# A hybrid mixer's values and keys turned to token order by VectorE's block transposes and transfers between partitions, in place of TensorE's transposes

## The chip, the core and the metric

The kernel runs on one core of one Trainium2 chip. The metric is the device time of one execution in microseconds (us). Three executions of the kernel before took 2284.95, 2286.54 and 2284.74 us; the median is 2284.95 us. The engines are called as in the profile: PE (TensorE, matmuls), PEld (its weight loads), DVE (VectorE), ACT (ScalarE), POOL (GpSimd) and SP (SyncE, which here only issues transfers).

## The reference

One step of a hybrid decoder layer for 256 new prompt tokens and 8 sample sequences of 4 tokens each, so 288 token columns. The model width is 2048. Every sub-layer is added to x:

```
x = x + 1/2 * post1(SwiGLU_1(pre1(x)))
x = x + post2(HybridMixer(pre2(x)))
x = x + 1/2 * post3(SwiGLU_2(pre3(x)))
```

The mixer multiplies its input by one large weight matrix, whose columns are split into queries, keys, values, decays and gates of two groups of heads: GLA (4 heads, 128 key and 256 value dimensions) and HGRN (8 heads, 128 and 128). Each head runs a linear recurrence:

```
S_t = diag(a_t) S_{t-1} + k_t^T v_t ;  o_t = q_t S_t
...
s_new = (jnp.exp(last[:, :, 0, :])[..., None] * s
         + jnp.einsum('bhsd,bhsv->bhdv', ki * jnp.exp(last - cum), vi))
```

The prompt begins from a zero state and each sample from a state that is given. The outputs are the new x for all tokens, and the final states of the prompt and of every sample. What matters for this change: the products need values `v` and keys `k` with the *token* on the partitions (the sum over tokens is the matmul's contraction), while the projection leaves them with the *feature* on the partitions. So values and keys have to be turned.

## The kernel before, in words

Activations lie transposed: a tile has 128 features on its partitions and 288 token columns (columns 0 to 255 are the prompt, 256 to 287 the samples). Weights stream from HBM as fp32 in units of 128 x 1024 elements (512 KB) through the class `Weights`: SP issues the load into one of three raw buffers (`RAW_BUFS`), ACT copies the unit to a rounded high part `wh` (line 95), DVE subtracts for the low part `wl` (line 96), and four such pairs are kept (`HL_BUFS`). A weight block of 128 x 128 takes three matmuls (lines 520, 521 and 522). The function `block` computes 512 output features from 16 contraction steps; one step is 4 x 3 = 12 matmuls, a block 192. After each step it calls `tick`, which may put other work into PE's stream; when a block ends, its four results are evacuated by the function `evac`.

There are three phases: the first SwiGLU (0 to 853 us of the profiled span), the mixer (854 to 1421) and the second SwiGLU (to the end). In the mixer the blocks come in this order: `qk0`, `v0`, `qk1`, `v1` (GLA's two pairs of heads), `hfq0`, `hi0`, `hfq1`, `hi1`, `hfq2`, `hfq3` (HGRN: decays and queries, and values), the gates, and the output projection `mo`. While they run, six scans (g0 and g1 of GLA, h0 to h3 of HGRN, each for two heads) go along as Python generators: `tick` steps the generator at the head of the list `gens` once per contraction step, and scans come one after another. A scan first works out decayed scores level by level, then turns keys (`key_t`, `key_e`), makes the prompt's output (`out`), the prompt's final state (`final`: matmuls on line 1108, a copy on ACT, line 1110, and a POOL transfer, line 1111), and goes through the samples (`halve`, `apart`, `sample`; the sample states leave by POOL, line 1147), then adds the parts up (`inter_a`, `inter_b`) and normalises (`norm_a` to `norm_c`).

The values' evacuation `ev_v` before: for each of the four results f, two DVE operations (lines 831 and 832) scale the prompt's columns into a tile y and the samples' columns, three times over, into a tile v3. A function `turn` is put on the list `turns`, which `tick` empties one at a time: it does three PE transposes by `by_token` (lines 810 and 811) into a PSUM tile `tp_v`, an ACT copy into `Vt` (line 839: prompt values by token, 128 tokens x 2), one into `V32` (line 840: the 32 sample tokens), and `stack` (an ACT copy, line 815, and a DVE subtraction, line 817) into `Vs`, which holds the sample values as high, low and high parts in its 96 partitions. Keys go the same way in `key_t` (three transposes into `tp_k`) and `key_e` (an ACT copy into `kd`, line 1076, and `stack` into `ks`).

The order of instructions on each engine is set when the program is built: a scheduler places them by priority and by a planner's costs, and `issue_after` pins some behind others. Transfers issued by SP and POOL each go round eight semaphores: a transfer waits until the one issued eight before it on the same queue has landed. Auxiliary PSUM tiles (`tp_v`, `tp_k`, `st` and the scores) share three buffers.

## Time and profile before

| | before |
|---|---|
| median of three executions | 2284.95 us |
| profiled execution, its own time | 2287.87 us |
| span of the profiled execution | 2286.1 us |
| granted TensorE clock (1 is full speed) | 0.998 |
| PE busy over the span | 2270.9 us (99%) |
| DVE / ACT / POOL busy | 1409.7 / 1045.5 / 57.5 us |
| mixer window, 854 to 1421: PE, DVE, ACT, POOL busy | 564.3, 450.0, 334.9, 44.9 us |

The profile is one execution. Its page gives the busy time of each engine, the busy share in 40 slices, the chain of work that ended last (followed back from the last instruction, by share of engine), and groups of instructions by line. A row of a group reads: line, engine, operation, output<-input by the program's names, shapes and count | busy us, mean ns of one | idle time of the engine just before them and what ended it. A row of a timeline reads: start in us, duration in us, engine, line, operation, names, shapes, count; where PE's matmuls overlap, their starts tell the pace. A row of the waits reads: engine, the waiting tile and line, what it waited for, us in total, times, longest.

### The profile page before, as it was taken

The page shows a single profiled execution, that of the slowest core. Times are in us where ns is not written, and L with a number is a line of the kernel's source. Part 1 is how long each engine was busy: PE and PEld are TensorE (multiplying, and loading weights), DVE is VectorE, ACT ScalarE, POOL GpSimd, SP SyncE. Part 2 cuts the span into 40 slices and gives each one's busy share as a digit, 9 for nine tenths or more (in the row PEclk, how much of TensorE's full clock was granted, in tenths as well). Part 3 has the DMA queues.
Part 4 walks back from the last instruction along what each step waited for, and adds up shares of the span by engine and source line. Part 5 has one row for each costly group of instructions (what it writes and reads, how often), then busy time and mean ns, then how long its engine had stood idle before and what let it go on. Part 6 is the DMA issues. An engine that isn't in the chain of part 4 may idle for free.

```text
span 2286.1 us, 42014 instructions
## 1 busy us (share of the span) xinstructions
PE 2270.9 (99%) x17224; PEld 2257.6 (99%) x17224; DVE 1409.7 (62%) x2319; ACT 1045.5 (46%) x1654; POOL 57.5 (3%) x104
## 2 busy tenths in 40 slices
PE   9999999999999999999999999999999999999998
PEld 9999999999999999999999999999999999999998
DVE  6545545554555468889889754844555455545545
ACT  6443333333334346555666654644333333333345
POOL 0000000000000002001000000100000000000000
PEclk9999999999999999999999999999999999999999
DMA  7555555555556545456565554455555555555553
GB/s 213 171 165 166 165 167 164 167 166 167 165 166 185 166 157 169 138 171 191 151 177 164 162 184 155 141 171 166 164 167 164 169 161 166 166 163 163 165 165 115
DMA packets 218560, 378.28 MB, mean 165 GB/s; under 512 B 15634, under 2 KB 55104, under 8 KB 218368
## 3 DMA queue, kind: packets, MB, share of 16 engines
q1 hardware_dynamic: 212560, 365.48, 53.4%
q0 software_dynamic: 3632, 9.94, 1.3%
q8 instruction: 135, 2.21, 0.4%
q10 hardware_dynamic: 2176, 0.18, 0.1%
q14 instruction: 57, 0.47, 0.1%
HBM read 363.75 MB, written 11.80 MB: 164 GB/s over the span
## 4 chain that ended last, share of the span: by engine, by line
PE 94%; DVE 3%; ACT 1%; DMA 1%; issue 0%; DVEq 0%; ACTq 0%; SPq 0%
PE gate L522 9%; PE gate L520 9%; PE gate L521 9%; PE up L522 8%; PE up L520 8%; PE up L521 8%; PE out L521 8%; PE out L522 8%; PE out L520 8%; PE hfq L520 2%; PE hfq L522 2%; PE mo L522 1%; PE mo L520 1%; PE mo L521 1%; PE hfq L521 1%; PE v L520 1%
## 5 line engine op out<-in xcount | busy, mean ns | idle before, releaser
L96 DVE TENSOR_TENSOR wl<-raw,wh 128x1024 fp32r<-128x1024 f32 (+1 forms) x674 | 821.9, 1220 | 631.8 <-ACT wh L95 629.7
L95 ACT ACTIVATE wh<-raw 128x1024 fp32r<-128x1024 f32 (+1 forms) x674 | 711.3, 1056 | 1018.4 <-PE gate L521 312.4
L520 PE MATMUL gate<-xh,wh 128*128 128x288 f32 x1660 | 489.2, 296 | 0.9 <-ACT wh L95 0.9
L522 PE MATMUL gate<-xh,wl 128*128 128x288 f32 x1660 | 489.0, 295 | 0.2 <-DVE wl L96 0.2
L521 PE MATMUL gate<-xl,wh 128*128 128x288 f32 x1660 | 485.6, 295 | 0.6 <-DVE xl L253 0.6
L521 PE MATMUL out<-hl,wh 128*128 128x288 f32 x1408 | 415.8, 295 | 0.0
L520 PE MATMUL out<-hh,wh 128*128 128x288 f32 x1408 | 415.6, 295 | 0.0
L522 PE MATMUL up<-xh,wl 128*128 128x288 f32 x1408 | 415.1, 295 | 0.0
L522 PE MATMUL out<-hh,wl 128*128 128x288 f32 x1408 | 414.9, 295 | 0.0
L520 PE MATMUL up<-xh,wh 128*128 128x288 f32 x1408 | 414.8, 295 | 0.1
L521 PE MATMUL up<-xl,wh 128*128 128x288 f32 x1408 | 414.6, 294 | 0.0
L520 PEld LDWEIGHTS gate<-xh,wh 128*128 128x128 f32 x1660 | 310.9, 188 | 1.8 <-ACT wh L95 1.1
L522 PEld LDWEIGHTS gate<-xh,wl 128*128 128x128 f32 x1660 | 311.5, 188 | 0.6 <-DVE wl L96 0.6
L521 PEld LDWEIGHTS gate<-xl,wh 128*128 128x128 f32 x1660 | 310.4, 188 | 1.0 <-DVE xl L253 0.8
L522 PEld LDWEIGHTS out<-hh,wl 128*128 128x128 f32 x1408 | 264.7, 188 | 0.0
L520 PEld LDWEIGHTS out<-hh,wh 128*128 128x128 f32 x1408 | 264.6, 188 | 0.0
L520 PEld LDWEIGHTS up<-xh,wh 128*128 128x128 f32 x1408 | 264.1, 188 | 0.5 <-ACT g L590 0.3
L521 PEld LDWEIGHTS out<-hl,wh 128*128 128x128 f32 x1408 | 264.5, 188 | 0.0
L521 PEld LDWEIGHTS up<-xl,wh 128*128 128x128 f32 x1408 | 264.2, 188 | 0.1
L522 PEld LDWEIGHTS up<-xh,wl 128*128 128x128 f32 x1408 | 264.2, 188 | 0.0
L650 DVE TENSOR_TENSOR y<-out,y 128x288 f32<-128x288 f32 x288 | 121.6, 453 | 104.2 <-PE out L522 101.4
L520 PE MATMUL hfq<-xh,wh 128*128 128x288 f32 x256 | 77.5, 303 | 0.0
(381 smaller groups left out, 2558.6 us busy)
## 6 DMA issues: line engine op xcount, KB each, us to landing
raw<-in_ffn_w_in_dram SPq DMA_DIRECT2D x351, 512.0 KB, 3.6
raw<-in_ffn_w_out_dram SPq DMA_DIRECT2D x176, 512.0 KB, 3.8
raw<-in_mix_w_in_dram SPq DMA_DIRECT2D x64, 512.0 KB, 3.7
raw<-in_mix_w_in_dram SPq DMA_DIRECT2D x96, 256.0 KB, 3.3
raw<-in_mix_w_out_dram SPq DMA_DIRECT2D x32, 512.0 KB, 3.8
out_dram<-s POOLq DMA_DIRECT2D x32, 256.0 KB, 3.4
s<-in_state_gla_dram SPq DMA_DIRECT2D x16, 256.0 KB, 4.4
s<-in_state_hgrn_dram SPq DMA_DIRECT2D x16, 256.0 KB, 3.4
```

Of the source, the lines that this page charges most:

```text
L95: i1 = self.nc.scalar.activation(h[:, c], raw[:, c], AF.Copy).ins
L96: i2 = self.nc.vector.tensor_tensor(l[:, c], raw[:, c], h[:, c].bitcast(F32), op=ALU.subtract).ins
L520: yield lambda: PE.matmul(dst, w[0][:, c:c + P], parts[0], start=start, stop=False)
L521: yield lambda: PE.matmul(dst, w[0][:, c:c + P], parts[1], start=False, stop=False)
L522: yield lambda: PE.matmul(dst, w[1][:, c:c + P], parts[0], start=False, stop=stop)
L650: V.tensor_tensor(y[k], ps, y[k], op=ALU.add)
```

## The change

Three things change.

1. Values. The sixteen y tiles become four groups of four (`yg`), so that the four results of a value block lie in one tile of 128 x 4 x 288. `ev_v` scales each result with one DVE operation. At the fourth it transposes the whole group in place in 32 x 32 blocks on DVE, and issues 36 transfers within the chip's own memory (18 on SP's queue, 18 on POOL's): for each of four blocks of partitions one into `V32` and eight into `Vt`, each moving 32 partitions x 4 x 32 elements in pieces of 128 bytes. The three PE transposes and the copies from PSUM go. The list `turns` gets two empty entries and one `turn` for the block, which makes `Vs` from `V32` with two ACT copies and a DVE subtraction of 32 x 512.
2. The prompt's keys. `keys_by_token`, called once in a scan behind `key_t(0)`, transposes both heads' keys in place on DVE (2 x 256 columns) and issues 32 POOL transfers into one `kd` tile. `key_t` keeps only the transpose for the samples' keys, and the ACT copy into `kd` goes.
3. The final states. `final(0)` and `final(1)` move from the first sample step of each head to the scan's end, behind `inter_a(1)` and `norm_a(1)`.

Over the whole program PE loses 72 transposes of 128 x 128 or 128 x 96 (48 `tp_v`, 24 `tp_k`); SP issues 72 more transfers and POOL 264 more.

```
-    y = [xpool.tile([P, T], F32, name=f"y{k}") for k in range(KT)]
+    yg = [xpool.tile([P, 4, T], F32, name=f"y{k}") for k in range(4)]
+    y = [yg[k // 4][:, k % 4, :] for k in range(KT)]
...
-            def ev_v(Vt, V32, Vs, y0=8):
+            def ev_v(Vt, V32, Vs, g=2):
+                vg = yg[g]
                 def ev(f, ps):
-                    vt = y[y0 + f]
-                    v3 = tmp.tile([P, 3, TS], F32, name="v3", tag="v3", bufs=4)
-                    V.tensor_tensor(vt[:, 0:TP], ps[:, 0:TP], rt[:, 0:TP], op=ALU.mult)
-                    V.tensor_tensor(v3, ps[:, TP:T].unsqueeze(1).broadcast_to([P, 3, TS]),
-                                    rt[:, TP:T].unsqueeze(1).broadcast_to([P, 3, TS]), op=ALU.mult)
-                    def turn():
-                        tp = auxtile("tp_v")
-                        by_token(tp, vt, v3.rearrange("p n t -> p (n t)"))
-                        c = slice(f * P, (f + 1) * P)
-                        S.activation(Vt[:, 0:2, c], tp[:, 0:TP].rearrange("p (t c) -> p t c", c=P), AF.Copy)
-                        S.activation(V32[0:TS, c], tp[0:TS, TP:TP + P], AF.Copy)
-                        stack(Vs[:, c], tp, TS)
-                    turns.append(turn)
+                    V.tensor_tensor(vg[:, f, :], ps, rt, op=ALU.mult)
+                    if f == 3:
+                        V.transpose(vg, vg)
+                        for b in range(4):
+                            rows, cols = slice(b * TS, (b + 1) * TS), slice(b * TS, (b + 1) * TS)
+                            queue = nc.sync if b % 2 else G
+                            queue.dma_start(V32[0:TS].rearrange("p (f c) -> p f c", c=P)[:, :, cols], vg[rows, :, TP:T])
+                            for t in range(2):
+                                for c in range(4):
+                                    c0 = t * P + c * TS
+                                    queue.dma_start(Vt[c * TS:(c + 1) * TS, t].rearrange("p (f c) -> p f c", c=P)[:, :, cols],
+                                                    vg[rows, :, c0:c0 + TS])
+                        turns.append(lambda: None)
+                        turns.append(lambda: None)
+                        turns.append(turn)
+                def turn():
+                    v = V32[0:TS, :]
+                    S.activation(Vs[0:TS, :], v, AF.Copy)
+                    V.tensor_tensor(Vs[TS:2 * TS, :], v, Vs[0:TS, :].bitcast(F32), op=ALU.subtract)
+                    S.activation(Vs[2 * TS:96, :], v, AF.Copy)
                 return ev
...
+                def keys_by_token():
+                    V.transpose(k[:, :, 0:TP], k[:, :, 0:TP])
+                    kd = sp[0].tile([P, 2, 2, P], F32, name="kd", tag="kd", bufs=1)
+                    for a in range(2):
+                        for b in range(4):
+                            src = k[b * TS:(b + 1) * TS, a, 0:TP].rearrange("p (t q c) -> p t q c", t=2, q=4)
+                            for c in range(4):
+                                G.dma_start(kd[c * TS:(c + 1) * TS, a, :, b * TS:(b + 1) * TS], src[:, :, c, :])
+                    return kd
                 def key_t(a):
                     tp = auxtile("tp_k")
-                    by_token(tp, k[:, a, :], K3[:, a].rearrange("p n t -> p (n t)"))
+                    PE.transpose(tp[0:96, TP:TP + P], K3[:, a].rearrange("p n t -> p (n t)"), ident)
                     return tp
                 def key_e(a, tp):
-                    kd = sp[0].tile([P, 2, P], F32, name="kd", tag="kd")
                     ks = sp[0].tile([96, P], F32R, name="ks", tag="ks")
-                    S.activation(kd, tp[:, 0:TP].rearrange("p (t c) -> p t c", c=P), AF.Copy)
                     stack(ks, tp, 2 * TS)
-                    kds[a] = kd, ks
+                    kds[a] = None, ks
...
                 tp = key_t(0)
+                kd = keys_by_token()
                 halve(0, 0)
...
-                        if b0 == 0:
-                            final(a)
                         sample(a, b0)
...
                     inter_a(a)
+                    if a == 1:
+                        final(0)
                     yield
                     inter_b(a)
                     norm_a(a)
+                    if a == 1:
+                        final(1)
```

More of the change, by code (lines that the diff above doesn't have):

```diff
@@ L1103, in final @@
                 def final(a):
-                    kd, vc = kds[a][0], Vt[:, :, a * dv:(a + 1) * dv]
+                    vc = Vt[:, :, a * dv:(a + 1) * dv]
                     ps = auxtile("st")
                     for t in range(2):
-                        PE.matmul(ps[:, 0:dv], kd[:, t, :], vc[:, t, :], start=t == 0, stop=t == 1)
+                        PE.matmul(ps[:, 0:dv], kd[:, a, t, :], vc[:, t, :], start=t == 0, stop=t == 1)
                     st = tmp.tile([P, dv], F32, name="st", tag="st", bufs=1)
@@ L1334, in mixer @@
                     vts[g] = vtiles(f"h{g}")
-                    block(f"hi{g}", KT, xrhs, ev_v(*vts[g], 8 + 4 * g), tick=tick)
+                    block(f"hi{g}", KT, xrhs, ev_v(*vts[g], 2 + g), tick=tick)
                 else:
```

## The prediction

> **What bounds the kernel now.** I read the page's busy totals first, then its chain, then the windows of the three phases, and last PE's own timeline around the steps that the change touches.

> ```profile
> span 2286.1 us, 42014 instructions
> PE 2270.9 (99%) x17224; PEld 2257.6 (99%) x17224; DVE 1409.7 (62%) x2319; ACT 1045.5 (46%) x1654; POOL 57.5 (3%) x104
> PE 94%; DVE 3%; ACT 1%; DMA 1%; issue 0%; DVEq 0%; ACTq 0%; SPq 0%
> ```

> PE is busy all through, and 94% of the chain that ended last is PE: the kernel is the sum of its matmuls. The next view gives each phase (first SwiGLU, mixer, second SwiGLU) by engine: PE, PE's weight loads, DVE, ACT, POOL.

> ```profile
> 0.00:853.00 853.00, 850.20 (x6403) 848.90 (x6404) 478.07 (x667) 351.60 (x446) 3.40 (x14) 1.00 0.57 171
> 854.00:1421.00 567.00, 564.31 (x4361) 554.69 (x4362) 449.99 (x975) 334.86 (x714) 44.86 (x71) 1.00 0.56 167
> ```

> VectorE is 79% busy in the mixer against 56% in the phase before. In the mixer PE idles under 3 us of 567, DVE has 117 us idle, ACT 232, POOL nearly everything. A change there can win only PE time that it removes, and lose whatever it makes PE wait for. PE's timeline (start, duration) shows what a turn of values costs:

> ```profile
> 918.68 0.29 PE L520 MATMUL qk<-xh,wh 128*128 128x288 f32 x1
> ...
> 919.47 0.38 PE L810 MATMUL tp_v<-ident,y 128*128 128x128 f32 x2
> 919.69 0.27 PE L811 MATMUL tp_v<-ident,v 128*96 128x128 f32 x1
> 919.72 0.38 PE L520 MATMUL qk<-xh,wh 128*128 128x288 f32 x1
> 919.93 0.30 PE L521 MATMUL qk<-xl,wh 128*128 128x288 f32 x1
> ```

> Starts count, since matmuls overlap. Six ordinary matmuls take 919.47 − 918.68 = 0.79 us, 0.132 each. The three transposes hold PE for 0.25 us (919.47 to 919.72), and the ordinary matmul behind them takes 0.21 to its successor, 0.08 too long: 0.33 us for a turn.

> ```profile
> 1085.94 0.38 PE L810 MATMUL tp_k<-ident,k_h 128*128 128x128 f32 x2
> 1086.15 0.27 PE L811 MATMUL tp_k<-ident,acc 128*96 128x128 f32 x1
> 1086.26 0.39 PE L1095 MATMUL o<-Dg,Vh 128*128 128x128 f32 x2
> ```

> A turn of keys: 0.32 us for three, of which the L810 pair (1085.94 to 1086.15) is 0.21 and the third, which stays, 0.11.

> **The change, part by part.**

> *PE.* 16 value turns (4 blocks by 4) go: 16 × 0.33 = 5.3 us. 12 key turns lose two of three: 12 × 0.21 = 2.5 us. Together 7.8 us, all on the bound. Bounds: from the durations, 48 tp_v records are 7.92 us busy and 36 tp_k 5.91 us (two thirds 3.9), which overlap each other; so above 11.8 us nothing, and by starts alone without the slow follower 4.0 + 2.5 = 6.5. I take 7.8. The `st` matmuls only move.

> *DVE and ACT.* These groups (count | busy, mean ns) carry the removed and the nearest added work:

> ```profile
> L831 DVE TENSOR_TENSOR y<-hi,rt 128x256 f32<-128x256 f32 x8 | 3.3, 418 | 0.0
> L832 DVE TENSOR_TENSOR v<-hi,rt 128x96 f32<-128x96 f32 x8 | 2.0, 251 | 0.0
> L817 DVE TENSOR_TENSOR Vsh<-tp_v,Vsh 32x128 fp32r<-32x128 f32 x8 | 2.3, 284 | 1.2 <-ACT Vsh L815 1.0
> L1297 DVE TENSOR_TENSOR z<-hfq,rt 128x288 f32<-128x288 f32 x16 | 7.1, 451 | 2.4 <-PE hfq L522 2.3
> L96 DVE TENSOR_TENSOR wl<-raw,wh 128x1024 fp32r<-128x1024 f32 (+1 forms) x674 | 821.9, 1220 | 631.8 <-ACT wh L95 629.7
> L839 ACT ACTIVATE Vh<-tp_v 128x256 f32<-128x256 f32 x8 | 3.0, 371 | 0.4 <-PE tp_v L811 0.3
> L840 ACT ACTIVATE vs<-tp_v 32x128 f32<-32x128 f32 x16 | 4.0, 251 | 0.0
> L815 ACT ACTIVATE Vsh<-tp_v 96x128 fp32r<-96x128 f32 x8 | 2.0, 252 | 0.0
> L1076 ACT ACTIVATE kd<-tp_k 128x256 f32<-128x256 f32 x12 | 4.5, 373 | 3.4 <-PE tp_k L811 3.4
> ```

> DVE loses 16 × (0.418 + 0.251 + 0.284) = 15.2 us and gains 16 evacuations of 128x288 at 0.451 = 7.2. No row shows a 32x32 block transpose. Its lower bound is L1297's slope: 32 columns more than L831 cost 33 ns, so 1152 columns 1.3 us and 512 columns 0.65; L96 gives 1.2 us per 1024 likewise. The upper bound is the small-operand price: 36 blocks and 16 blocks at L832's 251 ns each, 9 and 4 us. Being one instruction over a whole row of columns it is nearest to L96, so I take 1.4 us (four) and 0.65 (six), 9.5 us together, and four subtractions of 32x512 at about 0.65, 2.6. DVE: −15.2 + 7.2 + 9.5 + 2.6 = +4.1 us of 117 idle; at the upper bound +55. [...] ACT loses 16 × 0.874 + 12 × 0.373 = 18.5 and gains eight copies of 32x512 at some 0.6: −13.7. Neither is on PE's path.

> *DMAs.* Each of four value blocks sends 18 on SP's queue and 18 on POOL's; each of six scans sends 32 on POOL's. Rows for the issue cost, and for landing (KB each, us):

> ```profile
> 0.74 0.43 SPq L276 DMA_DIRECT2D xin<-in_x_prompt_dram  x1
> L1147 POOL DMA_DIRECT2D out_dram<-s x32 | 23.5, 733 | 62.6 <-DVE s L1145 52.8 <-DMA raw<-in_mix_w_in_dram 7.3 <-DVE k_h L1308 1.9
> L1111 POOL DMA_DIRECT2D out_dram<-st x12 | 6.6, 553 | 272.3 <-ACT st L1110 183.6 <-ACT hl L1122 71.8 <-DMA raw<-in_mix_w_in_dram 8.7
> 880.13 3.83 POOL L776 DMA_DIRECT2D y<-in_gla_w_gate_up_dram  x8 [21.16 <-DVE x L492]
> 884.53 2.02 POOL L776 DMA_DIRECT2D y<-in_gla_w_gate_up_dram  x4 [0.56 <-DMA y<-in_gla_w_gate_up_dram]
> out_dram<-st POOLq DMA_DIRECT2D x8, 64.0 KB, 2.0
> araw<-in_mix_w_in_dram ACTq DMA_DIRECT2D x1, 128.0 KB, 7.3
> ```

> POOL: 0.48 each in a burst (3.83 / 8), 0.55 once the ninth waits for the first to land (884.53 − 880.13 over 8). I take 0.55, the bounds being 0.48 and L1147's 0.733. So 18 take 9.9 us and 32 take 17.6. Landing: 2.0 (st) to 7.3 (the 128 KB load in small pieces); I take 2.5, nearest to the 16 KB pieces of `st`'s kind. SP: 18 × 0.43 = 7.7 us per block, ahead of the next weight load. What covers it: a split unit of 1024 columns feeds 24 matmuls, 24 × 0.132 = 3.2 us, and four split buffers (HL_BUFS) hold 12.7 us, three raw ones another 9.5. So 0 here, and 7.7 per block if those buffers happened to be empty.

> *The new waits.* (a) Values. In before the last evacuation of v0 is at 916.80 (L832), so the transpose is done near 918.5, and the tenth POOL DMA, the last that V32 needs, is issued by 924.0 and lands at 926.5. The third turn asks for it on ACT near 924.4. Behind it on ACT is the scan's R (L893), and behind that PE's first scores:

> ```profile
> 916.80 0.25 DVE L832 TENSOR_TENSOR v<-v,rt 128x96 f32<-128x96 f32 x1
> 924.37 0.36 ACT L839 ACTIVATE Vg<-tp_v 128x256 f32<-128x256 f32 x1
> 925.06 0.47 ACT L893 ACTIVATE R<-Q 128x288 f32<-128x288 f32 x1
> 928.75 0.94 PE L901 MATMUL sc<-R,k_g 128*128 128x128 f32 x7
> ```

> ACT stalls 2 us, makes two copies (1.2) and R (0.5): ready at 928.2, while PE, without four turns, asks at 928.75 less four turns of 0.33, 927.4. Stall 0.8; bounds 0 (landing 1.7 sooner) and 6 (landing 7.3). The other three blocks ask later after their evacuation; 0.2 together. (b) Keys. `final` moves to the scan's end, where kd is now asked. In the built order 122, 140, 149 and 168 ordinary matmuls lie between tp_k and the second `st` of h0 to h3, with some 5 us of scan matmuls among them: 21.0, 23.4, 24.6 and 27.1 us; for g0 and g1 far more. kd is there after 1.5 (DVE) + 32 × 0.55 + 2.5 = 21.6. Stall 0.6 at h0, none elsewhere. At 0.48 none at all; at 0.733 ready at 27.5, stalls 6.5 + 4.1 + 2.9 + 0.4 = 13.9. (c) State outputs (L1147) stand behind 32 key DMAs on POOL, up to 17 us late; the next state loads on SP wait for them and weight loads behind those. The buffers above hold 22 us: 0, and 5 if they are short. (d) The 4.1 us more of DVE come in front of R and masks: taken as 0.8 in all. The rows that PE already loses to such a feeder, and one that vanishes:

> ```profile
> PE sc L965 <- DVE R L958: 0.7, 1, 0.7
> PE tp_v L810 <- DVE y L831: 0.3, 1, 0.3
> ```

> **Sum:** −7.8 − 0.3 + 0.8 + 0.2 + 0.6 + 0.8 = −5.7 us. The profiled execution took 2287.87 us (span 2286.1 and 1.8 around it), 2.9 over the median 2284.95; so 2282.2 for such an execution, and 2279.2 for a median; I say 2279.5. A measurement tells from no change about 0.2%, 4.6 us: this is just beyond it.

> **Rivals.** *R1, slower: POOL's issue.* 264 more DMAs go through a queue that had about 60. If one costs 0.733 as L1147's rows do, the kd waits are 13.9 us and the V32 wait of g0 grows by 10 × 0.18 = 1.8; 2284.95 − 5.7 − 0.6 + 13.9 + 1.8 = 2294. It decides for slower near 0.70, and at 0.9 gives 2313. For it: L1147 itself, and DVE 79% busy beside it. Against: L1111's twelve are all near 553 under the same DVE, and a key DMA has 64 pieces where that has 128. [...] *R2, nothing left:* landing near 5 instead of 2.5 and DVE's transposes at 4 times the price make V32 4 us late in g0 and 2 in each of two other blocks, kd 2.5 late in h0 and 0.5 in h1: −7.8 − 0.3 + 0.8 + 8 + 3 = +3.7 at worst, 2288.7; with half of these waits −1.8, 2283.2. For it araw's 7.3, against it st's 2.0. *R3, clean:* every wait hidden, −8.1, 2276.9.

> **Chances.** Forecast (2278 to 2281) 0.38, R3 0.14, R2 0.24, R1 and other lateness of weights 0.24. Faster by over 0.2% means under 2280.4: R3, and three quarters of the forecast, and a little of R2: 0.45. Slower means above 2289.5: most of R1 and some of R2: 0.26. Same: 0.29. The range runs from R3's 2276.5 to 2300, into R1; the forecast's own is 2276.5 to 2283.

> **What would show it.** Right: no tp_v in PE's timeline, tp_k single, PE's mixer window shorter by about 6 us; POOL's key bursts of 32 in 16 to 18 us; ACT's R of g0 waiting for V32 by 1 to 2 us. Wrong: waits `st` from a DMA, of 3 us and more, would mean R1; waits for `wh` or `wl` in the mixer, that SP's queue was not covered; DVE's transposes far over 1.4 us, R2.

## The result, and the profile after

The changed kernel took 2310.16 us (median of four, 2309.74 to 2311.53) against 2285.26 us before (four executions here too): a ratio of 1.011 (95% interval 1.0098 to 1.0122). It is 25 us slower, where 5.7 us less were forecast. The first lines of the page after:

```profile
span 2307.7 us, 42237 instructions
PE 2275.6 (99%) x17152; PEld 2260.4 (98%) x17152; DVE 1413.7 (61%) x2301; ACT 1038.2 (45%) x1602; POOL 199.3 (9%) x368
PE 88%; DMA 3%; POOL 3%; DVE 2%; issue 2%; ACT 1%; SPq 1%; DVEq 0%; ACTq 0%; POOLq 0%
```

72 matmul instructions are gone, yet PE is busy 4.7 us *longer*; its share of the chain fell from 94 to 88%, and DMA, POOL and SP's queue have come into it. The same 567 us of the kernel after come next (PE, weight loads, DVE, ACT and POOL as in the prediction; the last three columns are the granted clock, the busy share of the DMA engines and GB/s). Then come PE's longest waits over the whole run (waiting line, what it waited for, us in total, times, longest), and last the longest wait of the kernel before:

```profile
854.00:1421.00 567.00, 545.60 (x4117) 533.91 (x4118) 444.69 (x947) 319.09 (x649) 186.23 (x333) 0.98 0.57 167
```

```profile
PE hms L1200 <- DVE s L1164: 4.9, 2, 3.9
PE sc L975 <- ACT R L969: 4.2, 2, 2.1
PE sc L911 <- ACT R L903: 3.4, 3, 2.6
PE st L1127 <- ACT st L1129: 3.0, 1, 3.0
PE sc L1005 <- DVE k_h L956: 1.5, 1, 1.5
```

```profile
PE v L520 <- ACT q_g L1263: 1.4, 1, 1.4
```

In the same 567 us PE gets 244 matmuls fewer done, 72 of which are the removed transposes, and its granted clock there is 0.98 instead of 1.00; the mixer ends some 21 us later. All waits of this view, without the one at the start of the program, sum to 21.3 us, against 4.3 before: 17 us more. The mean granted clock of the whole run is 0.993 against 0.998, and 0.005 of 2307.7 us is 11.5 us. That counts some time in which PE stood anyway: the trace's clock record has five stretches at half clock in the mixer, 23.9 us together, and PE had work in 21.4 of them, so they cost 10.7 us. With the 7.8 us that the prediction took as saved: 17 + 10.7 − 7.8 = 19.9, and the span grew by 21.6. So the loss has two parts: new waits, and a slower clock behind them. Both phases outside the mixer keep their pace (6408 matmuls against 6403 in the first 853 us, 6462 against 6457 in the last 865).

**Where the waits come from, first kind.** SP's queue behind the block v0, after and then before (start, duration, count):

```profile
908.00 2.57 SPq L61 DMA_DIRECT2D raw<-in_mix_w_in_dram  x3
916.62 0.74 SPq L839 DMA_DIRECT2D vs<-y  x1
917.41 5.09 SPq L843 DMA_DIRECT2D Vg<-y  x8
922.54 0.60 SPq L839 DMA_DIRECT2D vs<-y  x1
923.19 5.12 SPq L843 DMA_DIRECT2D Vg<-y  x8
928.41 2.06 SPq L61 DMA_DIRECT2D raw<-in_mix_w_in_dram  x4
```

```profile
909.43 13.71 SPq L61 DMA_DIRECT2D raw<-in_mix_w_in_dram  x8
926.55 4.79 SPq L63 DMA_DIRECT2D raw<-in_mix_w_in_dram  x2
```

The 18 transfers take 916.62 to 928.41, 11.8 us or 0.65 each, and no weight load is issued in that time, nor in the 6 us before, when SP waits for the transpose. On ACT this becomes:

```profile
924.49 0.63 ACT L851 ACTIVATE Vsg<-vs 32x512 fp32r<-32x512 f32 x1 [2.09 <-DMA vs<-y]
...
932.28 1.06 ACT L95 ACTIVATE wh<-raw 128x1024 fp32r<-128x1024 f32 x1 [3.27 <-DMA raw<-in_mix_w_in_dram]
933.25 0.40 ACT L969 ACTIVATE R<-Q 128x256 f32<-128x256 f32 x1
```

ACT stands 3.27 us at a split (L95) for a raw unit that is late. PE doesn't stand for that unit: its waits in the mixer have none for `wh` or `wl`. But the scan's R (L969, the queries laid out for the next scores) is next in ACT's queue, and PE stands 2.08 us for R.

**Second kind.** In the scan h3, after: POOL, then SP, ACT and PE (`hl` is the rounded copy of a sample's state, `st` a final state):

```profile
1230.92 4.80 POOL L1085 DMA_DIRECT2D kd<-k_h  x9 [0.60 <-DMA kd<-k_h]
1235.79 1.54 POOL L1166 DMA_DIRECT2D out_dram<-s  x2
...
1238.90 2.42 SPq L887 DMA_DIRECT2D s<-in_state_hgrn_dram  x3
...
1243.52 0.72 ACT L1141 ACTIVATE hl<-s 128x256 fp32r<-128x256 f32 x2 [4.39 <-DMA s<-in_state_hgrn_dram]
1244.15 0.26 ACT L1129 ACTIVATE st<-st 128x128 f32<-128x128 f32 x1
...
1244.46 0.91 PE L1127 MATMUL st<-Vh,kd 128*128 128x128 f32 x4 [3.04 <-ACT st L1129]
```

The key transfers end at 1235.7 and only then the states' outputs leave; SP, which reloads those buffers, waits until 1238.9; the state lands at 1243.5, where ACT has stood 4.39 us at `hl`; and the copy of `st` behind it holds PE 3.04 us.

**The clock.** Stretches of the kernel after (PE busy, clock, DMA share, GB/s), of 8 us around the stall near 931 us and the one near 1168, and then two of 3.41 us at the first:

```profile
928.00:936.00 8.00, 5.92 (x35) 0.89 0.71 209
936.00:944.00 8.00, 8.00 (x71) 0.90 0.63 190
1168.00:1176.00 8.00, 4.17 (x18) 0.61 0.90 255
```

```profile
930.81:934.22 3.41, 1.33 (x10) 1.00 1.05 341
934.22:937.63 3.41, 3.41 (x14) 0.50 0.63 190
```

PE is fully busy from 936 to 944, yet at 0.90: it runs at half clock from 934.22 to 937.63 and then at the full one again.

### The profile page after: what moved, and what is told of

It is laid out like the page before. It is cut to its first block, busy times and chain, and to the rows that moved or that the text cites. A ratio compares the mean times of both kernels' runs of the same rounds, so it can differ in the third digit from the quotient of the medians.

```text
span 2307.7 us, 42237 instructions
## 1 busy us (share of the span) xinstructions
PE 2275.6 (99%) x17152; PEld 2260.4 (98%) x17152; DVE 1413.7 (61%) x2301; ACT 1038.2 (45%) x1602; POOL 199.3 (9%) x368
## 4 chain that ended last, share of the span: by engine, by line
PE 88%; DMA 3%; POOL 3%; DVE 2%; issue 2%; ACT 1%; SPq 1%; DVEq 0%; ACTq 0%; POOLq 0%
PE gate L523 9%; PE gate L521 9%; PE gate L522 9%; PE up L523 8%; PE up L521 8%; PE up L522 8%; PE out L522 8%; PE out L523 8%; PE out L521 8%; POOL kd L1085 2%; PE mo L523 1%; PE mo L521 1%; PE mo L522 1%; DMA raw<-in_mix_w_in_dram 1%; SPq L843 1%
## 5 line engine op out<-in xcount | busy, mean ns | idle before, releaser
L96 DVE TENSOR_TENSOR wl<-raw,wh 128x1024 fp32r<-128x1024 f32 (+1 forms) x674 | 821.4, 1220 | 641.6 <-ACT wh L95 639.3
L95 ACT ACTIVATE wh<-raw 128x1024 fp32r<-128x1024 f32 (+1 forms) x674 | 711.1, 1056 | 1023.3 <-PE gate L522 314.2
L521 PE MATMUL gate<-xh,wh 128*128 128x288 f32 x1660 | 490.1, 297 | 0.1
L522 PE MATMUL gate<-xl,wh 128*128 128x288 f32 x1660 | 486.2, 295 | 0.0
L522 PE MATMUL out<-hl,wh 128*128 128x288 f32 x1408 | 415.8, 295 | 0.0
L521 PE MATMUL out<-hh,wh 128*128 128x288 f32 x1408 | 415.6, 295 | 0.0
L521 PE MATMUL up<-xh,wh 128*128 128x288 f32 x1408 | 414.8, 295 | 0.0
L522 PE MATMUL up<-xl,wh 128*128 128x288 f32 x1408 | 414.6, 294 | 0.0
L521 PEld LDWEIGHTS gate<-xh,wh 128*128 128x128 f32 x1660 | 311.7, 188 | 0.9 <-ACT wh L95 0.3
L522 PEld LDWEIGHTS gate<-xl,wh 128*128 128x128 f32 x1660 | 311.1, 188 | 0.4 <-DVE xl L254 0.2
L521 PEld LDWEIGHTS out<-hh,wh 128*128 128x128 f32 x1408 | 264.6, 188 | 0.0
L522 PEld LDWEIGHTS out<-hl,wh 128*128 128x128 f32 x1408 | 264.5, 188 | 0.0
L521 PEld LDWEIGHTS up<-xh,wh 128*128 128x128 f32 x1408 | 264.1, 188 | 0.2
L522 PEld LDWEIGHTS up<-xl,wh 128*128 128x128 f32 x1408 | 264.2, 188 | 0.1
L521 PE MATMUL hfq<-xh,wh 128*128 128x288 f32 x256 | 78.5, 307 | 0.0
```

Source lines behind the costliest of these rows:

```text
L95: i1 = self.nc.scalar.activation(h[:, c], raw[:, c], AF.Copy).ins
L96: i2 = self.nc.vector.tensor_tensor(l[:, c], raw[:, c], h[:, c].bitcast(F32), op=ALU.subtract).ins
L521: yield lambda: PE.matmul(dst, w[0][:, c:c + P], parts[0], start=start, stop=False)
L522: yield lambda: PE.matmul(dst, w[0][:, c:c + P], parts[1], start=False, stop=False)
```

## The experiments

Theory Q: the loss is one of queue order. Bursts of small transfers on SP and on POOL stand ahead of weight loads and of state outputs; ACT, in order, passes the lateness to PE, and the clock adds to it. Rivals: it is only the keys (K), only the values (V), the wait for what has landed (W), the late final states (F), or the transposes and traffic themselves wherever they are queued (T). In the code cuts − is a line taken out and + one put in, shortened at `...`, with remarks behind `#`; they are against the kernel after, and for the final states alone and the clock against the kernel before.

**One part alone: the values.**

```
-                kd = keys_by_token()
...
-                    PE.transpose(tp[0:96, TP:TP + P], K3[:, a].rearrange("p n t -> p (n t)"), ident)
+                    by_token(tp, k[:, a, :], K3[:, a].rearrange("p n t -> p (n t)"))
...
+                        if b0 == 0:
+                            final(a)
```

> Only the change to the values; keys and final states as before. Theory Q (queues): the 18 transfers of a value block on SP stand ahead of the weight loads, ACT waits in order at wh for a late raw unit with the scan's R behind it, and PE waits for R. In the trace of after the stalls of this kind, right behind the value blocks (near 925, 931, 1006, 1080, 1087 and 1168 us), sum to about 11 us, and the lower clock behind them takes 4 to 5 more; PE saves 5.3. So about 2285 - 5 + 11 + 4.5 = 2295, and a raw wait of ACT of 3 to 5 us behind each value block. Rival K (the keys and the moved final states cost it all, the values are harmless): 2280, and no such wait.

2299.42 us, ratio 1.0057 (1.004 to 1.0074): +13.3.

**One part alone: keys and final states.**

```
-                        V.transpose(vg, vg)
...
+                    def turn():
+                        tp = auxtile("tp_v")
+                        by_token(tp, vt, v3.rearrange("p n t -> p (n t)"))
```

> Only the keys by transfers and the final states at the scan's end; values as before. Theory Q: 32 POOL transfers of 0.54 us stand ahead of the sample states' outputs, so buffers for state loads come free 10 us and more later, SP's state loads are late, ACT stands at hl. Stalls of this kind in after (near 982, 992, 1051, 1123, 1199, 1241 us) sum to about 11 us, the clock adds 4, PE saves 2.5: 2297, with ACT waits at hl for state loads of 3 to 5 us. Rival K: 2310, all of the loss. Rival V (only the values cost): 2282.5.

2302.50 us, ratio 1.0072 (1.0057 to 1.0087): +16.4. Both parts lose, so K and V fall; singly they lose 29.7 us, together 25. The values-only kernel came 4.4 us and the keys-only kernel 5.5 us over what Q gave. ACT's waits for transfers in the mixer, in the kernel before, in the first kernel and in the second:

```profile
ACT wh L95 <- DMA raw<-in_mix_w_in_dram: 9.0, 4, 3.1
```

```profile
ACT wh L95 <- DMA raw<-in_mix_w_in_dram: 26.5, 11, 6.1
```

```profile
ACT hl L1131 <- DMA s<-in_state_hgrn_dram: 15.9, 4, 4.7
```

Each part makes its own wait, as Q says; before has no wait of `hl` for a state load in this view. But the longest PE stall of the values-only kernel, 3.1 us near 1157 at `os`, stands behind another: ACT waits 3.08 us for V32 itself, as W says.

**Values on POOL's queue.**

```
-                            queue = nc.sync if b % 2 else G
...
+                            G.dma_start(V32..., vg[rows, :, TP:T])      # V32's four first
...
+                                    G.dma_start(Vt..., vg[rows, :, c0:c0 + TS])
```

> As after, but all 36 transfers of a value block go on POOL's queue, V32's four ahead; SP's queue carries none. Theory Q: the weight loads are on time again, ACT's waits at wh for raw behind the value blocks go, and with them the stalls near 931, 1006, 1087 and 1168 us, some 10 us with their clock; what the keys cost stays, and since POOL is 10 us longer busy behind hi1 some of it grows: about 2300. Rival W (the wait for landed values costs it, not SP's order): V32 lands some 5 us earlier here but Vt later, so at most 2 us better, 2308.

2307.26 us (1.0078 to 1.0109): 3 us better than after, not 10, and the two intervals overlap. ACT's raw waits did fall, from 20.6 to 10.6 us (9.0 in before), and the stalls near 1006 and 1168 us went; but POOL's burst of 20 us now stood ahead of the final states, which have one buffer:

```profile
ACT st L1130 <- DMA out_dram<-st: 15.5, 6, 4.6
```

This wait is 6.1 us in after. The lateness moved from one queue to the other. The total by itself would have spoken for W; the waits speak for Q. The same edit with keys and final states as before parts this:

```
-                kd = keys_by_token()
...
+                            G.dma_start(V32..., vg[rows, :, TP:T])      # and Vt's behind, all on POOL
```

> Values only, as in the values-only kernel (2299.4), but all 36 transfers in one burst on POOL, V32's four ahead, none on SP; keys, final states and the one st buffer as before. It parts SP's share from the rest. Theory Q: without transfers in front of the weights ACT's raw waits fall from 26.5 us to about 9, as in before, and the time to 2285.5 - 5.3 + 3 to 8 = 2283 to 2288, the rest being outputs behind POOL's burst of 20 us at hi1. If SP's order is not what costs, it stays at 2295 to 2300 with waits for V32 in front of PE's stalls.

2292.98 us, ratio 1.0033 (1.0021 to 1.0044). Raw waits fell from 26.5 to 7.8 us, as expected, and the time by 6.4 us, less than expected. What stays is a wait for V32 behind hi0 (ACT 4.6 us at `Vs`) and for states. So SP's order is about a third of the 13.3 + 5.3 us that the values lose. The rest is V32's lateness (W) and states behind POOL's burst; these runs don't part the two.

**Half of the key transfers.**

```
-                        for b in range(4):
+                        for b in range(4 if a == 0 else 0):
...
-                        PE.matmul(ps[:, 0:dv], kd[:, a, t, :], ...
+                        PE.matmul(ps[:, 0:dv], kd[:, 0, t, :], ...
```

> As after, but only the first head's 16 key transfers are issued in each scan; the second head's final state is made from the first head's keys (it leaves out the second head's turned keys). Theory Q: POOL's burst is 8.7 us instead of 17.4, the state outputs leave 8 to 9 us earlier, and most of the stalls near 1051, 1123 and 1241 us go: about 2310 - 9 = 2301. Rival F (the final states at the scan's end cost it, by the one st buffer and its transfer): they are all still there, so 2309 to 2310.

2294.94 us (1.0024 to 1.0054). This kernel leaves out the second head's turned keys. 15 us of the 25 are gone, more than Q's 9. The final states stand where they stood in after, so F falls as the main cause. Half of the traffic is gone too, so T needs the run with spread keys below. ACT's wait at `hl` for HGRN's states, in after and here:

```profile
ACT hl L1141 <- DMA s<-in_state_hgrn_dram: 10.4, 3, 4.4
```

```profile
ACT hl L1141 <- DMA s<-in_state_hgrn_dram: 2.9, 3, 1.4
```

**The final states alone moved.**

```
-                        if b0 == 0:
-                            final(a)
...
+                    if a == 1:
+                        final(0)
...
+                    if a == 1:
+                        final(1)
```

> The kernel before with its final states moved to the scan's end and nothing else: keys and values as before. Theory Q: the move alone costs nothing to 2 us, by the one st buffer (the second copy into it waits for the first transfer): 2285.5 to 2288. Rival F (the late final states are a main cost): 2292 or more, with ACT's waits at st in front of PE's stalls.

2288.39 us, ratio 1.0013 (1.0004 to 1.0021): 3.1 us, a little over Q's range and far under F's. ACT waits 7.3 us, in six times, for the first transfer to leave the one st buffer. PE's own waits in the mixer are 2.9 us against 2.4 before, so how these 3 us reach the time isn't shown.

**The keys spread over the steps.**

```
-                                G.dma_start(kd..., src[:, :, c, :])
+                                drip.append((kd..., src[:, :, c, :]))   # tick() issues two a step
...
+                    later.append([..., norm_b, norm_c] + ([final(0), final(1)] if a == 1 else []))
```

> As the keys-only kernel, with the 32 transfers of a scan spread over 16 steps and the final states four to six steps behind the scan's end; values as before. Theory Q: state outputs no longer stand behind a burst of 17 us, ACT's waits at hl go and with them the stalls near 1047, 1115, 1166 and 1234 us: 2285.5 - 2.5 + 0 to 2 = 2283 to 2285 against 2302.5. Rival F (the final states late in the scan and their one buffer cost it): 2298 or more, with PE waits at st.

2291.79 us (1.0016 to 1.004) against 2302.50 for the burst. So 10.7 us of the loss were the burst, with the same transposes and transfers, though the final states come four to six steps later here too. What is left, 5.8 us over before or 8.3 with the 2.5 that PE should save, is over Q's 0 to 2. The late final states may be 3 of it by the run above. One PE stall of 2.6 us is left, near 1112: POOL's last eight key transfers leave together (1100.64 to 1104.9) ahead of two state outputs, SP stands at a state load with weight loads behind it until 1108.0, and ACT waits 3.52 us at a split. ACT's raw waits are 18.8 us in this kernel, without any value transfer on SP, so they aren't a sign of the values alone.

**The values spread.** All on POOL, V32's at once and three more a step, two st buffers:

```
+                        for n in range(0, len(dmas), 3):
+                            turns.append(lambda n=n: some(n))           # three G.dma_start, and turn() at the sixth
```

> Values by block transposes and transfers as in the values-only kernel, but all 36 transfers on POOL: V32's four at once, the 32 others three at each contraction step, Vs made at the sixth step, two st buffers; keys and final states as before. Theory Q: SP's queue carries weights and states only, POOL's queue never holds an output back by more than 2 us, so the loss of the values-only kernel goes (2299.4): 2285.5 - 5.3 + 0 to 2 = 2280 to 2282. Rival T (the block transposes on DVE and the transfers' traffic cost it, wherever they are queued): 2292 to 2299.

2287.76 us, ratio 1.0008 (0.9999 to 1.0018): T falls as the main cause, as nearly all the loss of the values is gone with the same transposes and transfers; but it is 6 us over Q. One PE stall of 3 us is left, behind hi0, where V32 landed 4.5 us after ACT asked.

**Both spread:**

```
+                        for n in range(0, len(dmas), 3):
+                            turns.append(lambda n=n: some(n))
...
+                                drip.append((kd..., src[:, :, c, :]))
```

> As the spread values, and the keys' 32 transfers spread too, two at each contraction step, with the final states four to six steps behind the scan's end. Theory Q: the stalls of both kinds go, 2285.5 - 7.8 + 1 to 4 = 2279 to 2282; behind hi1 keys and values share POOL's queue for 25 us, where a stall of 1 to 3 us may stay. Rival T: 2300 or more.

2295.19 us (1.0025 to 1.0055), 14 us over Q. Where keys and values share POOL behind hi1, PE waits 4.3 us at `st` for `kd` itself. The forecast of a small rest was wrong: POOL is busy almost without a break from 1134 to 1180 us with these 68 transfers and the outputs between them.

**The values spread over both queues, Vs held back:**

```
+                            for i, (d, v) in enumerate(dmas[n:n + 4]):
+                                (nc.sync if i % 2 else G).dma_start(d, v)
...
+                    with tc.issue_after(product[0]):
+                        S.activation(Vs[0:TS, :], v, AF.Copy)
```

> Values only, spread: V32's four transfers on POOL at once, the other 32 four at each contraction step, two on SP and two on POOL, Vs held back to the eighth step, two st buffers; keys and final states as before. Theory Q: it is the burst in front of the weight loads that costs, not SP's transfers as such; two of 0.64 us in a step of 1.6 us let weights through. 2285.5 - 5.3 + 1 to 4 = 2281 to 2284, and no raw wait of ACT over 3 us behind the value blocks. If any value transfer on SP costs, it comes near the values-only kernel, 2295 or more.

2283.32 us against 2285.29, ratio 0.999 (0.998 to 0.9999): faster than the kernel before, by 2 us, with the values' half of the change. SP's queue behind v0 is now mixed:

```profile
917.83 2.03 SPq L848 DMA_DIRECT2D Vg<-y  x3
919.96 1.04 SPq L61 DMA_DIRECT2D raw<-in_mix_w_in_dram  x2
921.04 0.60 SPq L848 DMA_DIRECT2D Vg<-y  x1
921.74 1.05 SPq L61 DMA_DIRECT2D raw<-in_mix_w_in_dram  x2
```

ACT's raw waits are 9.5 us (26.5 in the values-only kernel, 9.0 in before). None lies in the some 50 us behind a value block, where the values-only kernel has 18.7, as expected; the longest, 3.6, comes after 1180 us. The granted clock is 0.999. So transfers on SP do no harm as such. This run changed the spreading, V32's queue, the place of Vs and the st buffers together, and doesn't part them.

**The clock by itself.**

```
+                    held = stall(STALLS[name]) if k == 8 and name in STALLS else None
+                    with tc.issue_after(held) if held else ExitStack():
                         for f in range(nf):
                             mm(w, f, k)
```

> The kernel before, with PE held four times in the first SwiGLU, far from the mixer: one small matmul, an ACT copy, 4, 10, 20 and 6 tiny POOL copies in a chain, and a matmul that waits for the last of them, ahead of the next ordinary one (16 small extra matmuls and copies in all, nothing left out). If a stall costs only itself, the time grows by the sum of the four gaps in PE's starts and the pace behind each is 0.132 us at a granted clock of 1.00. If the clock is taken down after a stall, as in after (granted 0.84 to 0.92 in 18 to 22 us around a stall of 2.3 to 4 us, none around two of 1.1 to 1.5), then each gap over some 2 us is followed by slower matmuls that cost 1 to 4 us more, and a short one is not.

2315.08 us, ratio 1.0129 (1.0111 to 1.0147): +29.1. Between ordinary matmuls the four gaps are 4.01, 5.64, 8.35 and 4.32 us; four paces of 0.13 off, they sum to 21.8. The next 24 matmuls lose 2.6, 2.5, 1.2 and 0.1 us more, matched start by start against the kernel before: 6.3, so 28.1 together. PE's pace behind the second stall, and the clock behind the first and the fourth:

```profile
344.20 0.44 PE L533 MATMUL up<-xl,wh 128*128 128x288 f32 x1
344.44 0.44 PE L534 MATMUL up<-xh,wl 128*128 128x288 f32 x1
```

```profile
184.00:188.00 4.00, 4.00 (x18) 0.50 0.13 49
...
666.00:670.00 4.00, 4.00 (x33) 1.00 0.05 18
```

Starts are 0.24 us apart instead of 0.13, at half the clock. A stall is thus followed by a loss of up to 2.6 us, but not always: 4.32 us cost next to nothing, 4.01 cost 2.6. The traces of after and of this kernel show a difference between them. In both the stretches at half clock, but for one at the program's end, begin whole multiples of 3.41 us apart (in after at 934.22, 1009.31, 1125.37, 1169.74 and 1244.83: 22, 34, 13 and 22 of them; here near 181.8, 342.2 and 502.7: 47 and 47) and last 3.41 or 6.83 us. The stall of 4.32 us falls on two such periods, the first two lines here, and PE is busy for about half of each; the third line follows at full clock:

```profile
659.65:663.06 3.41, 1.61 (x13) 1.00 0.53 169
663.06:666.47 3.41, 1.73 (x12) 1.00 0.52 176
666.47:669.88 3.41, 3.41 (x28) 1.00 0.00 0
```

By the gaps between PE's starts that are over 0.5 us, less a pace each, it stood for 0.57 and 0.49 of these two. In after it stood for 0.66, 0.67, 0.68, 0.59 and 0.89 of the five periods that end where a stretch at half clock begins, and for 0.45 at most of any other that ran at full clock in the mixer.

## Why the prediction was wrong, point by point

- *PE's saving.* All 72 transposes went. Its 7.8 us couldn't be read by itself. The version with values over both queues is 2 us under before with 2.2 us more of gaps in PE's starts (those over 0.5 us in the mixer, less a pace each, sum to 5.1 against 2.9), which shows some 4.2 of the 5.3 us for the values.
- *Prices.* Nearly all held. These rows of after answer the prices taken (1.4, 0.65, 0.65; POOL 0.55 and 0.55):

```profile
L835 DVE STREAM_TRANSPOSE y<-y 128x1152 f32<-128x1152 f32 x4 | 5.5, 1372 | 0.0
L1079 DVE STREAM_TRANSPOSE k_h<-k_h 128x512 f32<-128x512 f32 x4 | 2.8, 704 | 0.0
L852 DVE TENSOR_TENSOR Vsh<-vs,Vsh 32x512 fp32r<-32x512 f32 x2 | 1.4, 682 | 0.5 <-ACT Vsh L851 0.5
L1085 POOL DMA_DIRECT2D kd<-k_h x128 | 68.4, 543 | 102.4 <-PE os L1160 55.3 <-DVE ks L818 29.8 <-PE o L1116 16.4
L843 POOL DMA_DIRECT2D Vh<-y x32 | 17.4, 552 | 0.5 <-DMA vs<-y 0.4
```

  Median landings were 2.0 to 3.3 us where 2.5 were taken, and DVE's total rose by 4.0 us (forecast 4.1). SP's price was off: 0.65 us from start to start, not 0.43. ACT's total fell by 7.3 us, not 13.7; no run explains it.
- *(a) V32's wait in g0.* Right: ACT 2.09 us (forecast 2), PE's gap 0.86 where a pace is 0.13, so 0.7 (0.8). "The other three", 0.2: ACT waits 2.45 us in g1 too, but PE has no gap right behind it. That was partly luck: in the values-only kernel the wait behind hi1 is 3.08 us on ACT and 3.1 on PE.
- *(b) kd.* Right in that PE never waits for `kd` in after.
- *"What covers it ... So 0 here"* (SP's queue) is the first step that failed. The split buffers cover PE's need of weights: PE has no wait for `wh` or `wl` in the mixer, so the sign that the prediction named for an uncovered queue didn't come. They don't cover ACT, which makes the splits in order with the scan's own copies. The raw wait came earlier than PE's need of the unit, and R was behind it. With values alone, taking the transfers off SP brought back 6.4 us.
- *(c) "0, and 5 if they are short"* is the second. It named the right queues and the right order, and then let the same buffers hide it. The half-keys run shows 15 us for it and what follows from it, the run with spread keys 10.7.
- *"The `st` matmuls only move"* put the move at nothing; by itself it costs 3.1 us, in a way that isn't shown.
- *The clock* was left out of the sum altogether: 10.7 us of the 25, by the stretches at half clock.
- *R1.* The side and the queue were right, the mechanism wrong: a new transfer's issue on POOL took 0.54 to 0.56 us in the mean, beside a DVE that is 78% busy in the mixer. Nor did it take longer beside a block transpose: POOL issued three key transfers in 1.64 us from 1148.53 on in after, while DVE transposed values from 1148.60 to 1149.98. R1's 2313 for 0.9 us leaves out its own V32 term, with which it is some 2317; nothing hangs on it. R2 and R3 fall: transposes and landings cost what was forecast, and the waits stayed.

## What to carry to other kernels

The small transfers were paid here by what stood *behind* them in their queues (no weight load was issued on SP for the 11.8 us of 18 transfers): find the next instruction there, who waits for it, and what else is behind that waiter on its engine. The buffers protected the last consumer and not an engine in between: PE never waited for `wh` or `wl` in the mixer, while ACT stood 3.27 us at a split, with R behind it. Spreading six bursts of 32 transfers brought back 10.7 us of 16.4 here, and spreading four of 36 over both queues, with V32 first on POOL and Vs made later, all that the values had lost. Each stall of PE should be priced with the slower clock that may follow, 10.7 us of the 25 here; in after and in the run with four stalls that depended more on how much of one 3.41 us period the stall filled (0.59 to 0.89 with half clock behind it, 0.57 and 0.49 without) than on its length.
